# A two-layer hybrid decoder trunk: masked maxima in one operation, a planner with other durations, split weight tiles in places of 4352 bytes

## The chip, the core and the metric

The kernel runs on one core of a Trainium2 chip. The core has a matrix engine (PE; its weight loads are listed apart as PEld), a vector engine (DVE), an activation engine (ACT), a general engine (POOL) and a queue that starts transfers (SP). The metric is device time in microseconds, median of several runs. A profile of one execution gives times for every instruction; all rows below come from it.

## What is computed

```python
for i in range(DEPTH):                     # DEPTH = 2, SEQ = 256, D_MODEL = 1024, D_FF = 2816
    x = x + 0.5 * swiglu(rms_norm(x, ffn1_norm_g[i]), ffn1_w_in[i], ffn1_w_out[i])
    hn = rms_norm(x, mix_norm_g[i])
    if i % N_MIXERS == 0:
        proj = hn @ a_w_in[j]; y_tok = mlstm_heads(...)          # mixer A: 4 heads
    else:
        proj = hn @ b_w_in[j]; y_tok = swa_heads(...)            # mixer B: 16 heads of 64, 2 key heads
    y_mem = memory_heads(xq, mem_k, mem_v, ...)                  # 4 heads over 256 memory rows
    x = x + jnp.concatenate([y_tok, y_mem], axis=-1) @ w_out
    x = x + 0.5 * swiglu(rms_norm(x, ffn2_norm_g[i]), ffn2_w_in[i], ffn2_w_out[i])
```

The change touches the window heads of mixer B. In `swa_heads` each block of 128 queries sees its own keys and those of the block before it, under a mask, with one learned extra logit per head (the sink):

```python
s = jnp.where(valid, jnp.einsum('bqhgd,bkhd->bhgqk', qn, kn), -jnp.inf)
m = jnp.maximum(jnp.max(s, axis=-1, keepdims=True), sink)
p = jnp.exp(s - m)
denom = jnp.sum(p, axis=-1, keepdims=True) + jnp.exp(sink - m)
out = jnp.einsum('bhgqk,bkhd->bqhgd', p / denom, vn)
```

## The kernel before

**Products in three parts.** Every projection is made of float32 values split in a rounded high part and the rest. A weight tile (128 rows by 4 x 256 columns, 512 KB) is fetched by SP into one of five raw tiles `wr`; ACT makes its high part (`round`, line 312, tile `wh`), DVE the rest (`rest`, line 324, tile `wl`). `mm3` then issues high x high, high x low and low x high, 24 matmuls of 256 columns for a weight tile, all at line 456. A matmul has an operand that is loaded into the array (the weights of the instruction) and one that moves through it. In the feed-forward layers, the output projections and part of mixer A's input projection the weight tile is the loaded operand and the activations (`xh`, `xl`, or `u` tiles) move. In the memory stage at the start, in mixer B's input projection and where mixer A needs tokens in rows (`Group(rows=True)`, the gates), it is the other way round: activations are loaded and the weight tile moves.

**Where the tiles lie.** Pools are laid one after another in on-chip memory, in the order of their creation. Weight tile number i of the whole plan goes to pool `whp[i % 2]` and `wlp[i % 2]`, four places of 4096 bytes each; the small pool `gp` (two tiles of 64 bytes) stands between the pools of even and those of odd numbers. Eight temporaries `t` of 2048 bytes follow (pool `tp`).

**The order of the work.** All instructions of all five queues are put in order while the program is built (`manual_schedule`). A small planner, class `Weave`, holds a model clock `now` for PE and one for each other engine. The main line of the program is a generator that issues projection matmuls in pieces of six; everything else (norms, heads, activations) are generators, "chains", which tell by `yield` when they could go on. `pump` lets a chain go on if its time is at most 0.4 us (`LEAD`) ahead of `now`, or not ahead at all if its next step is a matmul. A class `Job` counts what a chain's steps cost: `dve`, `act`, `pool` and `pe`. The order so found is then fixed; on the chip each engine works through its queue and waits on semaphores where the model was wrong.

**A window head of mixer B** (`head`, from line 1422) handles two heads of 64 at once. Per pair it writes the mask into two banks by a bf16 product of an identity with the mask (line 1436, two matmuls of 384 columns), adds the scores on top (line 1441: four matmuls, each recorded as two), takes four negated maxima from the banks (lines 1446 and 1447), combines them with the negated sink (1451, 1452), makes four exponentials from the banks with their sums (1461), frees the banks, normalises (1466, 1467, 1473), transposes the probabilities (through line 470), copies them (1483) and multiplies with the values (1492). Eight such pairs run between the pieces of the projections.

Of the kernel before, what the change touches and what calls it, by code (L numbers as in the profile page):

```python
# [19 lines left out]
P = 128  # L20
# [99 lines left out]
class Job:  # L120


    def __init__(self, wv, *t):
        self.wv, self.eng, self.t = wv, None, max(t, default=wv.now + 0.32)
# [15 lines left out]
    def pe(self):  # L140

        self.wv.now += 0.12
        self.t, self.eng = self.wv.now + 0.3, "pe"
        return self.t
# [3 lines left out]
def tile_trunk(ctx: ExitStack, tc: tile.TileContext, a, out):  # L148
# [13 lines left out]
    mk(cst, [P, 16], F32, "pad")  # L162
# [85 lines left out]
    identb = mk(cst, [P, P], BF16, "identb")  # L248
# [3 lines left out]
    nsink = mk(cst, [P, 16], F32, "nsink")  # L252
# [5 lines left out]
    def late_constants():  # L258
# [8 lines left out]
        nc.vector.tensor_copy(identb, ident)  # L267
# [5 lines left out]
        nc.vector.tensor_scalar(nsink, sink, -1.0, None, op0=ALU.mult)  # L273
# [5 lines left out]
    class Stream:  # L279
# [14 lines left out]
        def fetch(self, i):  # L294
            src, shape, pre = self.plan[i]
# [13 lines left out]
        def round(self, i):  # L309
            shape, j = self.plan[i][1], Job(wv, self.landed[i])  # L310
            self.hi[i] = self.split(whp[i % 2], f"wh{i % 2}", shape)
            nc.scalar.copy(self.hi[i], self.raw[i])  # L312
            self.cast[i] = j.act(shape[1] * shape[2])

        def split(self, pool, tag, shape):

            if shape[2] == GATED:
                return mk(pool, [P, shape[1], 384], F32R, tag)[:, :, :GATED]
            return mk(pool, shape, F32R, tag)

        def rest(self, i):
            shape, j = self.plan[i][1], Job(wv, self.cast[i])
            self.lo[i] = self.split(wlp[i % 2], f"wl{i % 2}", shape)
# [50 lines left out]
    def cols(w, c0, kh):  # L374
        return chunks(w)[:, kh * 4:(kh + 1) * 4, c0:c0 + 256], [P, 4, 256], None

    def row(w, kc):
        return w[kc * P:(kc + 1) * P, :].rearrange("p (a b) -> p a b", a=4), [P, 4, 256], None
# [29 lines left out]
    def mem_plan():  # L408

        o = 0  # L410
        for i, (k0, nk, q0, nq) in enumerate(MEM_TILES):
# [4 lines left out]
            yield src, [P, nk, nq * T], None if pre is None else mem_in(*pre)  # L416

    def ffn_plan(w_in, w_out):
# [4 lines left out]
        for c2 in range(4):  # L423
            for k0, nk in KG:
                yield chunks(w_out)[:, k0:k0 + nk, c2 * 256:(c2 + 1) * 256], [P, nk, 256], None

    def mixer_plan(w, pair, rest, w_out, gates=None):
        for kh in range(2):
            for c0 in pair:
                yield cols(w, c0, kh)  # L430
        for c0 in rest:
            if c0 == gates:
                for k in range(0, 8, 2):
                    yield chunks(w)[:, k:k + 2, c0:c0 + GATED], [P, 2, GATED], None
                continue
            for kh in range(2):
                yield cols(w, c0, kh)
# [6 lines left out]
    for i, (src, shape, _) in enumerate(list(ffn_plan(a["ffn1_w_in"][0], a["ffn1_w_out"][0]))):  # L444
        plan.append((src, shape, x_in(i) if i < 2 else None))
    plan += mixer_plan(a["a_w_in"][0], A_PAIR, A_REST, a["a_w_out"][0], 3072)
    plan += ffn_plan(a["ffn2_w_in"][0], a["ffn2_w_out"][0])
    plan += ffn_plan(a["ffn1_w_in"][1], a["ffn1_w_out"][1])
    plan += mixer_plan(a["b_w_in"][0], B_PAIR, B_REST, a["b_w_out"][0])
# [37 lines left out]
    class Norm:  # L487
# [14 lines left out]
        def put(self, j, c2, xn):  # L502
            hi, lo = mk(xhp, [P, 2, T], F32R, "xh"), mk(xlp, [P, 2, T], F32R, "xl")
            for m in range(2):
                act(hi[:, m], xn[:, m], AF.Copy, scale=g(self.gi + 2 * c2 + m))  # L505
                j.act(T)
            yield j.t
            for m in range(2):
                stt(out=lo[:, m], in0=xn[:, m], scalar=g(self.gi + 2 * c2 + m), in1=hi[:, m].bitcast(F32),
                    op0=ALU.mult, op1=ALU.subtract)  # L510
                j.dve(T)
# [30 lines left out]
        def finish(self, j):  # L542
# [10 lines left out]
            if not self.rows:  # L553
# [5 lines left out]
                yield j.pe()  # L559
# [11 lines left out]
            yield j.pe()  # L571
# [146 lines left out]
    def memory():  # L718
# [73 lines left out]
        def keys(i):  # L792
# [6 lines left out]
            yield j.pe()  # L799
# [19 lines left out]
    def ffn(x, nxt=None, mid=None):  # L819
# [3 lines left out]
        def hidden(gi, bs):  # L823
# [3 lines left out]
            for m in range(2):  # L827
                tt(out=t[:, m], in0=bs[m].t[:, :T], in1=x.rb, op=ALU.mult)  # L828
                j.dve(T)
# [3 lines left out]
            for m in range(2):  # L833
                tt(out=t[:, m], in0=t[:, m], in1=bs[m].t[:, T:], op=ALU.mult)  # L834
                j.dve(T)
# [110 lines left out]
    def cross(src, banks, gi, layer, x, scales, ys, clear=lambda: True):  # L946
# [7 lines left out]
        yield j.pe()  # L954
# [5 lines left out]
        def head(m):  # L960
# [8 lines left out]
            yield j.pe()  # L969
# [3 lines left out]
            for h in range(2):  # L973
                act(p[:, h], sv[:, h], AF.Exp, bias=c[:, 2 + h:3 + h], accum_out=c[:, 4 + h:5 + h])
                j.act(T, True)
# [12 lines left out]
            yield j.pe()  # L988
# [8 lines left out]
            yield j.pe()  # L997
# [55 lines left out]
    def mixer_a(x, nxt):  # L1053
# [46 lines left out]
        def gates():  # L1100
# [15 lines left out]
            yield j.pe()  # L1116
# [40 lines left out]
            yield j.pe()  # L1157
# [24 lines left out]
        def decay(hd):  # L1182
# [24 lines left out]
            yield j.pe()  # L1207
# [30 lines left out]
        def numerators(hd, gr):  # L1238
# [21 lines left out]
            yield j.pe()  # L1260
# [29 lines left out]
            yield j.pe()  # L1290
# [81 lines left out]
    def mixer_b(x, nxt):  # L1372
# [5 lines left out]
        def keys(gr):  # L1378
# [15 lines left out]
            yield j.pe()  # L1394
# [9 lines left out]
        def queries(gi, gr):  # L1404
# [7 lines left out]
            yield j.pe()  # L1412
# [9 lines left out]
        def head(ch, qr):  # L1422
# [12 lines left out]
            for s in sc:  # L1435
                nc.tensor.matmul(s[:, :384], identb, maskb[:, :384], start=True, stop=False, skip_group_check=True)  # L1436
                wv.now += 0.16

            for cs, qs, ks in ((slice(0, P), slice(0, P), slice(0, P)), (slice(P, 384), slice(P, T), slice(0, T))):
                for e in range(2):  # L1440
                    nc.tensor.matmul(sc[e][:, cs], qr[es[e], m, qs], kd[es[e], jh, ks], start=False, stop=True,  # L1441
                                     skip_group_check=True)
                wv.now += (cs.stop - cs.start) * 0.0017
            yield j.pe()
            for e, s in enumerate(sc):
                nc.vector.tensor_reduce(out=c[:, e:e + 1], in_=s[:, :P], axis=AX.X, op=ALU.max, negate=True)
                nc.vector.tensor_reduce(out=c[:, 2 + e:3 + e], in_=s[:, P:384], axis=AX.X, op=ALU.max, negate=True)
                j.dve(P)
                j.dve(T)
# [128 lines left out]
```

## Time and profile before

| | |
|---|---|
| median of 3 runs | 995.66 us (994.76 to 995.8) |
| the profiled execution: its time, its span | 995.73 us, 994.0 us |
| PE busy, matmuls | 987.1 us (99%), 8531 |
| DVE, ACT, POOL busy | 680.0, 512.5, 53.7 us |
| transfers, busy share of 16 engines | 182.75 MB; 56.8% for the main queue |
| granted TensorE clock, mean | 1.000 |

The stages follow each other: memory (0 to 29 us), feed-forward (29 to 222), mixer A (222 to 326), two feed-forward layers (326 to 702), mixer B (702 to 810), feed-forward (to 990). In rows of the profile `bank<-wh,u` means: written is a bank of accumulators, the moving operand is `wh`, the loaded one `u`. A group's row gives the count after `x`, then the busy time and the mean duration in ns, then idle time of the engine before it and who ended it. A row of the timeline gives start, length (to the end of the last of its xN instructions), engine, line, and in brackets idle time before it. Matmuls overlap: one lasts some 277 ns, but a new one starts every 113 or so, so pace is read from starts.

### The profile page before, as it was taken

The numbers are of one execution on the slowest core, as the hardware profiler recorded it, in microseconds if no ns is written. First come the engines' busy times: TensorE is split into PE (matmuls) and PEld (weight loads), VectorE is DVE, ScalarE is ACT, GpSimd is POOL, SyncE is SP. The second block draws the span as 40 slices with busy tenths as digits, with TensorE's granted clock in tenths as the row PEclk, the third lists the DMA queues.
The fourth block names the chain that finished last, engine by engine and source line by source line (L and its number), as shares of the span: only waits on it lengthen the run. The fifth ranks groups of instructions, "written<-read, shape, count | busy, mean of one in ns | idle before, by whom it ended". The sixth has DMA issues, their size and how long they took to land.

```text
span 994.0 us, 20546 instructions
## 1 busy us (share of the span) xinstructions
PE 987.1 (99%) x8531; PEld 972.3 (98%) x8531; DVE 680.0 (68%) x1104; ACT 512.5 (52%) x778; POOL 53.7 (5%) x45
## 2 busy tenths in 40 slices
PE   8999999999999999999999999999999999999998
PEld 7999999999999999999999999999998899999998
DVE  7986666568767586666567776657688788776651
ACT  7754534447656464454444544445566765544440
POOL 1400000001001100000010000001122010000000
PEclk9999999999999999999999999999999999999999
DMA  9776565646455467656665657565523257666650
GB/s 338 223 252 203 172 192 190 190 133 213 145 170 162 156 211 234 192 179 187 195 221 167 198 182 232 171 209 168 185 86 102 95 166 226 219 196 206 192 171 23
DMA packets 169726, 182.75 MB, mean 184 GB/s; under 512 B 6076, under 2 KB 163952, under 8 KB 169632
## 3 DMA queue, kind: packets, MB, share of 16 engines
q1 hardware_dynamic: 168352, 179.63, 56.8%
q0 software_dynamic: 416, 0.75, 0.5%
q8 instruction: 67, 1.10, 0.4%
q10 hardware_dynamic: 864, 1.05, 0.3%
q14 instruction: 27, 0.22, 0.1%
HBM read 180.35 MB, written 1.05 MB: 183 GB/s over the span
## 4 chain that ended last, share of the span: by engine, by line
PE 98%; DMA 1%; ACT 0%; issue 0%; SPq 0%; DVE 0%; DVEq 0%; ACTq 0%
PE bank L456 92%; PE bank L465 2%; PE bank L470 2%; PE bank L1441 1%; PE bank L1492 1%; DMA wr<-in_a_w_in_dram 1%; DMA u<-in_mem_w_kv_dram 1%; PE bank L1436 0%; ACT wh L312 0%; SPq L385 0%; SPq L306 0%; DVE t L911 0%; ACT u L1108 0%; DVEq L1574 0%; ACTq L312 0%
## 5 line engine op out<-in xcount | busy, mean ns | idle before, releaser
L324 DVE TENSOR_TENSOR wl<-wr,wh 128x1024 fp32r<-128x1024 f32 (+1 forms) x346 | 404.5, 1208 | 50.8 <-ACT wh L312 49.5
L456 PE MATMUL bank<-xh,wh 128*128 128x256 f32 x1536 | 426.3, 278 | 0.0
L456 PE MATMUL bank<-xh,wl 128*128 128x256 f32 x1536 | 424.7, 277 | 0.0
L456 PE MATMUL bank<-xl,wh 128*128 128x256 f32 x1536 | 424.7, 277 | 0.0
L312 ACT CAST wh<-wr 128x1024 fp32r<-128x1024 f32 (+1 forms) x346 | 338.8, 1022 | 84.9 <-PE bank L456 48.5
L456 PE MATMUL bank<-u,wh 128*128 128x256 f32 x1792 | 308.3, 278 | 0.0
L456 PEld LDWEIGHTS bank<-xh,wh 128*128 128x128 f32 x1536 | 288.6, 188 | 0.1
L456 PEld LDWEIGHTS bank<-xl,wh 128*128 128x128 f32 x1536 | 288.5, 188 | 0.1
L456 PEld LDWEIGHTS bank<-xh,wl 128*128 128x128 f32 x1536 | 288.4, 188 | 0.0
L456 PEld LDWEIGHTS bank<-u,wh 128*128 128x128 f32 x1792 | 270.0, 188 | 1.7 <-issue 1.7
L456 PE MATMUL bank<-u,wl 128*128 128x256 f32 x896 | 247.9, 277 | 0.0
L456 PEld LDWEIGHTS bank<-u,wl 128*128 128x128 f32 x896 | 168.3, 188 | 0.0
L831 ACT ACTIVATE t<-t 128x512 f32<-128x512 f32 x44 | 27.8, 632 | 172.3 <-DVE t L828 171.7
L828 DVE TENSOR_TENSOR t<-bank,rb 128x256 f32<-128x256 f32 x88 | 35.9, 423 | 74.5 <-PE bank L456 74.5
L456 PE MATMUL bank<-wh,xh 128*128 128x256 f32 (+1 forms) x208 | 60.4, 290 | 0.0
L505 ACT ACTIVATE xh<-u,gcol 128x256 fp32r<-128x256 f32 x48 | 21.6, 501 | 71.3 <-DVE u L894 59.0
L456 PE MATMUL bank<-wl,xh 128*128 128x256 f32 (+1 forms) x208 | 58.2, 280 | 0.0
L456 PE MATMUL bank<-wh,xl 128*128 128x256 f32 (+1 forms) x208 | 58.1, 279 | 0.0
L535 POOL TENSOR_TENSOR u<-u,t 128x512 f32<-128x512 f32 x14 | 24.4, 1743 | 586.1 <-ACT t L532 585.9
L834 DVE TENSOR_TENSOR t<-t,bank 128x256 f32<-128x256 f32 x88 | 32.8, 418 | 24.9 <-ACT t L831 24.8
L891 DVE TENSOR_TENSOR t<-bank,hrb 128x512 f32<-128x512 f32 x12 | 8.3, 692 | 55.6 <-PE bank L456 55.6
L474 ACT CAST u<-t 128x512 fp32r<-128x512 f32 x44 | 27.4, 622 | 31.7 <-DVE t L834 23.3
(194 smaller groups left out, 664.9 us busy)
## 6 DMA issues: line engine op xcount, KB each, us to landing
wr<-in_ffn_w_in_dram SPq DMA_DIRECT2D x176, 512.0 KB, 5.1
wr<-in_ffn_w_out_dram SPq DMA_DIRECT2D x80, 512.0 KB, 4.8
wr<-in_a_w_in_dram SPq DMA_DIRECT2D x26, 512.0 KB, 5.0
wr<-in_b_w_in_dram SPq DMA_DIRECT2D x14, 512.0 KB, 4.9
wr<-in_a_w_out_dram SPq DMA_DIRECT2D x12, 512.0 KB, 4.1
wr<-in_b_w_out_dram SPq DMA_DIRECT2D x12, 512.0 KB, 3.3
wr<-in_ffn_w_out_dram SPq DMA_DIRECT2D x16, 256.0 KB, 3.0
wr<-in_mem_w_kv_dram SPq DMA_DIRECT2D x6, 512.0 KB, 7.0
```

The lines of the kernel that those rows point to most:

```text
L312: nc.scalar.copy(self.hi[i], self.raw[i])
L324: tt(out=self.lo[i], in0=self.raw[i], in1=self.hi[i].bitcast(F32), op=ALU.subtract)
L456: nc.tensor.matmul(ps, lhsT, rhs, start=start, stop=stop, skip_group_check=True)
L465: nc.tensor.matmul(ps, lhsT, rhs, start=start, stop=stop, skip_group_check=True)
L470: nc.tensor.transpose(ps, src, ident[:k, :k])
L474: nc.scalar.copy(hi, src)
L505: act(hi[:, m], xn[:, m], AF.Copy, scale=g(self.gi + 2 * c2 + m))
L535: nc.gpsimd.tensor_tensor(out=self.acc, in0=self.acc, in1=sq, op=ALU.add)
L828: tt(out=t[:, m], in0=bs[m].t[:, :T], in1=x.rb, op=ALU.mult)
L831: act(t, t, AF.Silu)
L834: tt(out=t[:, m], in0=t[:, m], in1=bs[m].t[:, T:], op=ALU.mult)
L1441: nc.tensor.matmul(sc[e][:, cs], qr[es[e], m, qs], kd[es[e], jh, ks], start=False, stop=True, skip_group_check=True)
```

## The change

1. **Window heads.** The two mask matmuls go; the first score matmul of a bank starts it. One DVE operation per block (`tensor_tensor_reduce`) adds the mask, writes the masked scores to the tile that will hold the probabilities, and gives their maximum. The banks are freed at once and the exponentials read that tile. The maxima are no longer negated, so the sink is used as it is and one small operation turns the sign. The tiles `identb` and `nsink` and the two operations that fill them go.
2. **Places of the split weights.** Eight pools of one place each for `wh` and eight for `wl`, tile i in place i % 8; a place is 1088 words (4352 bytes), and the tile starts 32 or 64 words into it, by the parity of i and by whether the plan marks the tile as moving. Six temporaries `t` instead of eight, `gp` moved behind them, and the padding after `onesr` 96 words instead of 16.
3. **The planner.** Other durations for DVE and ACT; a step that depends on the one before pays `HOP` (0.04) on its own engine too, one that does not (`dep=False`) nothing; `pe` adds what its caller gives, from 0.0 to 0.4, instead of 0.12.

```diff
-    def use(self, eng, cost):
-        start = max(self.wv.clock[eng], self.t + (0.0 if eng == self.eng else HOP))
-        self.wv.clock[eng], self.t, self.eng = start + cost, start + cost + 0.08, eng
+    def use(self, eng, cost, dep=True):
+        start = max(self.wv.clock[eng], self.t + HOP if dep else 0.0)
+        self.wv.clock[eng], self.t = start + cost, start + cost + 0.08
         return self.t
-    def dve(self, n=8):
-        return self.use("dve", 0.08 + n * 0.00103)
-    def act(self, n=8, total=False):
-        return self.use("act", 0.14 + n * 0.00092 + 0.09 * total)
+    def dve(self, n=8, dep=True):
+        return self.use("dve", 0.07 + n * 0.00104, dep)
+    def act(self, n=8, total=False, dep=True):
+        return self.use("act", 0.13 + n * 0.0008 + 0.09 * total, dep)
-    def pe(self):
-        self.wv.now += 0.12
+    def pe(self, more):
+        self.wv.now += more
...
-    mk(cst, [P, 16], F32, "pad")
+    mk(cst, [P, 96], F32, "pad")
...
-    whp, wlp = [pool("whp0", 4)], [pool("wlp0", 4)]
+    whp = [pool(f"whp{i}", 1) for i in range(8)]
+    wlp = [pool(f"wlp{i}", 1) for i in range(8)]
+    tp = pool("tp", 6)
+    sp = pool("sp", 2)
     gp = pool("gp", 1)
-    whp.append(pool("whp1", 4))
-    wlp.append(pool("wlp1", 4))
-    tp = pool("tp", 8)
-    sp = pool("sp", 2)
...
+        def split(self, i, pool, tag):
+            shape, moving = self.plan[i][1], self.plan[i][3]
+            n = shape[2] if shape[2] != GATED else 384
+            o = (32, 64)[i % 2] if not moving else (64, 32)[i % 2]
+            w = mk(pool[i % 8], [P, 1088], F32R, tag)[:, o:o + shape[1] * n].rearrange("p (a b) -> p a b", a=shape[1])
+            return w[:, :, :shape[2]]
...
-            yield j.pe()
+            yield j.pe(0.03)
...
-            for s in sc:
-                nc.tensor.matmul(s[:, :384], identb, maskb[:, :384], start=True, stop=False, skip_group_check=True)
-                wv.now += 0.16
...
-                    nc.tensor.matmul(sc[e][:, cs], qr[es[e], m, qs], kd[es[e], jh, ks], start=False, stop=True,
+                    nc.tensor.matmul(sc[e][:, cs], qr[es[e], m, qs], kd[es[e], jh, ks], start=cs.start == 0, stop=True,
                                      skip_group_check=True)
...
-            yield j.pe()
-            for e, s in enumerate(sc):
-                nc.vector.tensor_reduce(out=c[:, e:e + 1], in_=s[:, :P], axis=AX.X, op=ALU.max, negate=True)
-                nc.vector.tensor_reduce(out=c[:, 2 + e:3 + e], in_=s[:, P:384], axis=AX.X, op=ALU.max, negate=True)
-            snk = nsink[:, 2 * ch:2 * ch + 2].unsqueeze(1).to_broadcast([P, 2, 2])
-            tt(out=v22(c[:, 8:12]), in0=v22(c[:, 0:4]), in1=snk, op=ALU.min)
-            tt(out=v22(c[:, 12:16]), in0=v22(c[:, 8:12]), in1=snk, op=ALU.subtract)
+            yield j.pe(0.4)
+            p = [unit(F32).rearrange("p a b -> p (a b)") for _ in range(2)]
+            for e in range(2):
+                for h, cs in BLOCKS:
+                    nc.vector.tensor_tensor_reduce(
+                        out=p[e][:, cs], in0=sc[e][:, cs], in1=maskb[:, cs], scale=1.0, scalar=NEG,
+                        op0=ALU.add, op1=ALU.max, accum_out=c[:, 2 * h + e:2 * h + e + 1])
+                    j.dve(cs.stop - cs.start, e + h == 0)
+                bs[e].free()
+            snk = sink[:, 2 * ch:2 * ch + 2].unsqueeze(1).to_broadcast([P, 2, 2])
+            tt(out=v22(c[:, 8:12]), in0=v22(c[:, 0:4]), in1=snk, op=ALU.max)
+            tt(out=v22(c[:, 12:16]), in0=snk, in1=v22(c[:, 8:12]), op=ALU.subtract)
+            nc.vector.tensor_scalar(c[:, 8:12], c[:, 8:12], -1.0, None, op0=ALU.mult)
...
-                    act(p[e][:, cs], sc[e][:, cs], AF.Exp, bias=c[:, 8 + i:9 + i], accum_out=d[:, 4 + i:5 + i])
-                    j.act(cs.stop - cs.start, True)
-                bs[e].free()
+                    act(p[e][:, cs], p[e][:, cs], AF.Exp, bias=c[:, 8 + i:9 + i], accum_out=d[:, 4 + i:5 + i])
+                    j.act(cs.stop - cs.start, True, e + h == 0)
```

More of the change, by code (lines that the diff above doesn't have):

```diff
@@ L310, in round @@
             shape, j = self.plan[i][1], Job(wv, self.landed[i])
[L311 removed]
+            self.hi[i] = self.split(i, whp, "wh")
             nc.scalar.copy(self.hi[i], self.raw[i])
             self.cast[i] = j.act(shape[1] * shape[2])
[L315 to L319, printed above, removed]
+        def split(self, i, pool, tag):
[4 more added lines that the diff above has]
+            return w[:, :, :shape[2]]
         def rest(self, i):
             shape, j = self.plan[i][1], Job(wv, self.cast[i])
[L323 removed]
+            self.lo[i] = self.split(i, wlp, "wl")
             tt(out=self.lo[i], in0=self.raw[i], in1=self.hi[i].bitcast(F32), op=ALU.subtract)
@@ L433, in mixer_plan @@
                 for k in range(0, 8, 2):
-                    yield chunks(w)[:, k:k + 2, c0:c0 + GATED], [P, 2, GATED], None
+                    yield chunks(w)[:, k:k + 2, c0:c0 + GATED], [P, 2, GATED], None, True
                 continue
             for kh in range(2):
-                yield cols(w, c0, kh)
+                yield cols(w, c0, kh, moving)
         for kc in ORDER + LATE:
@@ L443, in tile_trunk @@
     plan = list(mem_plan())
-    for i, (src, shape, _) in enumerate(list(ffn_plan(a["ffn1_w_in"][0], a["ffn1_w_out"][0]))):
-        plan.append((src, shape, x_in(i) if i < 2 else None))
-    plan += mixer_plan(a["a_w_in"][0], A_PAIR, A_REST, a["a_w_out"][0], 3072)
+    for i, (src, shape, _, moving) in enumerate(list(ffn_plan(a["ffn1_w_in"][0], a["ffn1_w_out"][0]))):
+        plan.append((src, shape, x_in(i) if i < 2 else None, moving))
+    plan += mixer_plan(a["a_w_in"][0], A_PAIR, A_REST, a["a_w_out"][0], (3336, 1024, 1280, 1536, 1792), 3072)
     plan += ffn_plan(a["ffn2_w_in"][0], a["ffn2_w_out"][0])
     plan += ffn_plan(a["ffn1_w_in"][1], a["ffn1_w_out"][1])
-    plan += mixer_plan(a["b_w_in"][0], B_PAIR, B_REST, a["b_w_out"][0])
+    plan += mixer_plan(a["b_w_in"][0], B_PAIR, B_REST, a["b_w_out"][0], B_PAIR + B_REST)
     plan += ffn_plan(a["ffn2_w_in"][1], a["ffn2_w_out"][1])
@@ L1473, in head @@
                     nc.vector.tensor_scalar(p[e][:, cs], p[e][:, cs], d[:, 12 + i:13 + i], None, op0=ALU.mult)
-                    j.dve(cs.stop - cs.start)
+                    j.dve((cs.stop - cs.start) * 0.73, e + h == 0)
             yield from room(j, 2)
```

68 lines of the change are left out of this document (31 added, 37 removed).

## The prediction

> **What bounds the kernel now.** I read the page's head and chain first, then the windows by stage.
>
> ```profile
> span 994.0 us, 20546 instructions
> ...
> PE 98%; DMA 1%; ACT 0%; issue 0%; SPq 0%; DVE 0%; DVEq 0%; ACTq 0%
> ```
> ```profile
> 0.00:43.00 43.00, 40.41 (x322) 37.93 (x323) 35.08 (x59) 33.67 (x56) 13.79 (x15) 1.00 0.86 298
> ...
> 222.00:326.00 104.00, 103.44 (x835) 101.34 (x834) 76.51 (x153) 65.84 (x121) 7.62 (x9) 1.00 0.56 175
> ...
> 701.00:811.00 110.00, 110.00 (x911) 99.97 (x910) 86.44 (x231) 68.98 (x173) 13.91 (x8) 1.00 0.39 124
> ```
>
> The columns after the window's length are busy time of PE, PEld, DVE, ACT and POOL, then the granted clock. The chain is PE almost throughout, at full clock. PE idles 2.59 us of the first 43, 0.56 of mixer A (222 to 326) and nothing of mixer B (701 to 811). There is hardly a wait left to remove: only matmuls that are not issued, or issued closer together, shorten this kernel.
>
> How close they come differs by stage. The chain in order of time gives the feed-forward stages, the timeline of PE the memory stage:
>
> ```profile
> 46.24 175.13 PE bank L456 x1545
> ...
> 316.32 404.19 PE bank L456 x3560
> ...
> 797.94 192.36 PE bank L456 x1694
> ```
> ```profile
> 12.15 1.98 PE L456 MATMUL bank<-wh,u 128*128 128x256 f32 x16
> 13.97 1.07 PE L456 MATMUL bank<-wl,u 128*128 128x256 f32 x8
> 14.88 2.04 PE L456 MATMUL bank<-wh,u 128*128 128x256 f32 x16
> 16.77 1.10 PE L456 MATMUL bank<-wl,u 128*128 128x256 f32 x8
> 17.71 1.98 PE L456 MATMUL bank<-wh,u 128*128 128x256 f32 x16
> 19.53 1.07 PE L456 MATMUL bank<-wl,u 128*128 128x256 f32 x8
> 20.43 2.05 PE L456 MATMUL bank<-wh,u 128*128 128x256 f32 x16
> ```
>
> The operand named first after the arrow moves, the second is loaded as weights. With the weight tile loaded (xh,wh and u,wh) a matmul follows each 175.13/1545 = 113.4 ns. With the weight tile moving (wh,u) it depends on the tile: 24 matmuls take 14.88 - 12.15 = 2.73 us in one tile, 17.71 - 14.88 = 2.83 in the next, 2.72 in the third. Tiles of even number take longer than those of odd number, by 0.10 us a tile or 4.2 ns a matmul. Same shapes, same clock, no idle time: what alternates with a tile's number is its pool, whp[i % 2], and so its start address.
>
> **The change: the mask.** Line 1436's two matmuls a head go.
>
> ```profile
> 741.17 0.28 PE L456 MATMUL bank<-wh,xl 128*128 128x256 f32 x1
> ...
> 742.59 0.50 PE L1436 MATMUL bank<-maskb,identb 128*128 128x384 bf16 x2
> 743.01 0.93 PE L1441 MATMUL bank<-u,u 64*128 64x128 f32 x8
> ```
> ```profile
> 757.18 0.28 PE L456 MATMUL bank<-wl,xh 128*128 128x256 f32 x1
> 757.30 0.28 PE L456 MATMUL bank<-wh,xl 128*128 128x256 f32 x1
> 757.51 0.87 PE L1492 MATMUL bank<-t,u 128*64 128x256 f32 x8
> ```
>
> From 742.59 to 743.01 they hold PE for 0.42 us. Not all of it goes: a matmul on part of the array comes late after one on the whole of it (757.30 to 757.51 is 0.21, where 0.12 is usual), and the scores at line 1441 use 64 rows, so these 0.09 us stay. Eight heads by 0.33 us give **2.7 us**; if the 0.09 went too it would be 3.4, and I take 2.6 as the low end. PE has no idle time there, so all of it shortens the span.
>
> **The mask's other side.** The maxima move to an operation that adds the mask, takes the maximum and writes the masked scores.
>
> ```profile
> L1447 DVE TENSOR_REDUCE col<-bank 128x1 f32<-128x256 f32 x16 | 6.6, 415 | 0.0
> ...
> L1446 DVE TENSOR_REDUCE col<-bank 128x1 f32<-128x128 f32 x16 | 4.6, 286 | 3.6 <-PE bank L1441 3.4
> ...
> L689 DVE TENSOR_SCALAR col<-col,qsc 128x4 f32<-128x4 f32 x8 | 1.4, 224 | 0.0
> ```
> ```profile
> L602 DVE CUSTOM_DVE_ANT_0 t<-rb,con x2: 286/287/288, 221.7 to 221.9; 128x128 f32<-128x128 f32 x2
> L602 DVE DVE_READ_ACCUMULATOR2_ANT rc<- x2: 82/82/82, 221.9 to 222.1; 128x1 f32 x2
> ```
> ```profile
> L828 DVE TENSOR_TENSOR t<-bank,rb 128x256 f32<-128x256 f32 x88 | 35.9, 423 | 74.5 <-PE bank L456 74.5
> ...
> L505 ACT ACTIVATE xh<-u,gcol 128x256 fp32r<-128x256 f32 x48 | 21.6, 501 | 71.3 <-DVE u L894 59.0
> ```
>
> On 128 columns it took 287 + 82 = 369 ns where the reduction takes 286. On 256 from PSUM it is not in this trace: at least 423 + 82 = 505 (a two-input operation of that size plus the accumulator's read), at most twice 369 = 738; I take 505 against 415. With the added sign change at 224 a head costs DVE 2 x 0.083 + 2 x 0.090 + 0.224 = 0.57 us more (at most 1.04), 4.6 in all (8.3). Mixer B leaves DVE 23.6 us idle, but order counts, so look at the wait behind it:
>
> ```profile
> 791.11 1.01 DVE L1473 TENSOR_SCALAR u<-u,col 128x128 f32<-128x128 f32 x4
> ```
> ```profile
> 793.96 0.82 PE L470 MATMUL bank<-con,u 128*128 128x128 f32 x6
> ...
> 797.07 0.87 PE L1492 MATMUL bank<-t,u 128*64 128x256 f32 x8
> 797.87 0.50 PE L456 MATMUL bank<-u,wh 128*128 128x256 f32 x2
> ```
>
> These probabilities are ready at 792.12 and PE turns to them at 793.96, 1.84 us later, filled with output-projection matmuls. A head 0.57 (or 1.04) later still finds cover; without it, eight heads would cost 4.6 us. The last head has more: behind 797.87 come 108 projection matmuls up to 810.4, the last 48 alone needing heads 6 and 7. The exponentials reading SBUF instead of PSUM cost ACT about nothing (501 ns for 256 columns from SBUF); two banks come free before them instead of behind. I cost this part at **0**. The two small operations dropped at the start are off the path.
>
> **The places.** The sizes of the pools give the starts. Modulo 512 bytes a weight tile starts at 0 (even) or 128 (odd) now, the activations at 448. A place becomes 4352 bytes, 256 more than before, so with the offsets of 32 or 64 words a loaded weight tile starts at 128 (even) or 0 (odd), a moving one at 256 or 384. Moving start less loaded start: moving weights had 0 - 448 = 64 (the tiles of 2.83 us) and 128 - 448 = 192 (those of 2.73); loaded weights have 448 and 320, both of which run at 113.4 ns through the 1545 matmuls above. After, moving weights get 256 - 448 = 320 and 384 - 448 = 448, the two that run well today; loaded weights keep 448 and 320. The padding keeps the activations where they are.
>
> ```profile
> L456 PE MATMUL bank<-wh,xh 128*128 128x256 f32 (+1 forms) x208 | 60.4, 290 | 0.0
> ```
> ```profile
> L456 PE MATMUL bank<-wh,u 128*128 128x256 f32 x128 | 17.3, 284 | 1.4 <-ACT wh L312 1.4
> ```
>
> Three products of 208 in the mixers and, one and a half times 128, 192 in the memory stage are 816 matmuls, 34 tiles of 24; the 17 even ones lose 17 x 0.10 = 1.7 us. That is the most to gain; the most to lose is the other 17 turning to that pace, again 1.7. Between interruptions by the heads a stretch need not find the better pace at once, so I take **1.0**, a part of the gain.
>
> Here the Trainium skill speaks against the change. TensorE: Matmul & The Clock Gate, "Step-by-step: what each phase is for", says that PE has two independent SBUF read ports and that loading the next weights takes nothing from the running matmul. By it the places would be worth nothing and the sum would be 993.0; the 2.83 and 2.73 us of neighbouring tiles do not agree with it.
>
> **Six temporaries.** The tightest reuse that I find six places apart is in the memory stage:
>
> ```profile
> 25.33 1.78 DVE L538 TENSOR_TENSOR u<-u,t 128x512 f32<-128x512 f32 x1
> ```
> ```profile
> 29.98 0.62 ACT L532 ACTIVATE t<-u 128x512 f32<-128x512 f32 x1
> ```
>
> The old user ends at 27.11, the new one begins at 29.98: 2.9 us of room, cost **0**.
>
> **The planner's durations** reorder the queues. Turning to a chain counts 0.02 or 0.03 us of PE time instead of 0.12, a dependent step on the same engine 0.04 more than before. Mixer A is where it could hurt:
>
> ```profile
> 248.25 1.07 ACT L990 COPY t<-bank 128x512 f32<-128x512 f32 x2 [1.29 <-PE bank L470]
> ```
> ```profile
> 249.12 0.38 PE L465 MATMUL bank<-t,vM 128*128 128x256 f32 x1
> ```
> ```profile
> 230.01 0.45 PE L470 MATMUL bank<-con,u 128*36 128x128 f32 x2 [0.56 <-ACT u L1108]
> ```
>
> The matmul at 249.12 has half of its input ready only since about 248.8. Eight such turns a quarter of a microsecond late would cost 2 us; the 0.56 us stall at 230.01 may vanish. Bounds -0.6 and +2, value **0**, since the two edits pull in opposite directions.
>
> **The sum** is made against the profiled execution: 995.73 us, 994.0 of span and 1.7 around it, 0.07 above the median of 995.66. 995.73 - 2.7 - 1.0 = **992.0**.
>
> **Rivals.** *Only the mask pays*: if starts count modulo 256 and not by distance, moving weights at 256 and 384 behave as at 0 and 128: 993.0. For it: nothing in this trace starts at 256 modulo 512. Against: distance sorts all four cases seen. *More than forecast*: the whole 3.4 and 1.7, the 0.56, and the 1.21 us that PE waits at 7.85 for its second tile: 988.9. *The planner takes back part*: 2 us of new turns, 994.0, or somewhat more. *Slower*: the feed-forward stages fall into the pace of 2.83 us a tile. They are 1545 + 3560 + 1694 = 6799 matmuls; at 4.2 ns half of them would cost 14 us, 1006. Against it: their distances do not change, only even and odd swap. It decides once some 57 tiles of 24 run so (57 x 0.10 is over the 3.7 saved plus 2).
>
> ```profile
> 7.85 1.22 PE L456 MATMUL bank<-wh,u 128*128 128x256 f32 x8 [1.21 <-ACT wh L312]
> ```
>
> **Chances.** Forecast 0.46, mask alone 0.21, more 0.10, planner's loss 0.15, slower 0.08. This kernel's measurement can tell about 0.2% (2 us) from no change: below 993.7 is faster, above 997.7 slower. The forecast and "more" are faster, of mask alone most (0.17); with rounding faster 0.73, same 0.19, slower 0.08. The range is 988.9 to 996.0: low end the larger gain, high end the planner's loss with the moving tiles' 1.7 lost too (995.73 - 2.7 + 2 + 1.7 = 996.7, cut to 996.0 as all at once is unlikely).
>
> **What would show it.** Line 1436 gone and 0.33 us less from a projection matmul to the first score; the memory tiles all near 2.73 us; feed-forward at 113.4 ns; PE idle in 701 to 811 still near zero although DVE has 4 to 5 us more. Wrong if a tile at 256 or 384 still takes 2.83, if transposes of the probabilities wait for DVE, or if mixer A shows new idle time on PE.

## The result, and the profile after

The changed kernel takes 998.00 us (median of 9 runs, 996.83 to 998.75) against 995.51 us of the kernel before (9 runs beside them, 994.73 to 995.92). The ratio is 1.0026, with a 95% interval of 1.0017 to 1.0035: slower by a quarter of a per cent, where 992.0, a gain of 3.7 us, was forecast. The profiled execution took 997.94 us. Its page begins:

```profile
span 996.2 us, 20547 instructions
## 1 busy us (share of the span) xinstructions
PE 985.2 (99%) x8515; PEld 972.1 (98%) x8515; DVE 682.1 (68%) x1142; ACT 513.8 (52%) x778; POOL 51.6 (5%) x45
```

PE is busy 1.9 us less than before (987.1), and the span is 2.2 us longer. So PE stands idle 4.1 us more. The windows of the same three stages say where (columns as before: length, busy PE, PEld, DVE, ACT, POOL, granted clock):

```profile
0.00:43.00 43.00, 39.67 (x319) 37.07 (x320) 34.56 (x56) 33.15 (x56) 14.69 (x18) 1.00 0.83 283
...
222.00:326.00 104.00, 104.00 (x843) 102.14 (x842) 76.80 (x155) 66.56 (x122) 8.38 (x9) 1.00 0.54 173
...
701.00:811.00 110.00, 106.02 (x871) 97.68 (x870) 85.53 (x266) 68.73 (x168) 12.14 (x8) 0.98 0.38 122
```

Mixer B, where PE had no idle time at all, now has 3.98 us of it, and its clock is no longer 1.00. Mixer A lost its 0.56 us stall. In the first 43 us PE idles 3.33 us instead of 2.59; new there is one wait, not in the memory stage but behind it, in the first feed-forward layer, where a sum waits for a `u` tile that DVE makes late:

```profile
32.13 0.62 PE L455 MATMUL bank<-onesr,u 128*128 128x256 f32 x3 [0.81 <-DVE u L475]
```

The timeline of PE in the changed kernel shows the waits of mixer B (in brackets: idle time before the row, and who ended it):

```profile
771.96 0.28 PE L455 MATMUL bank<-u,wl 128*128 128x256 f32 x1
772.16 1.58 PE L1437 MATMUL bank<-u,u 64*128 64x128 f32 x16
773.68 0.50 PE L455 MATMUL bank<-u,wh 128*128 128x256 f32 x2
...
775.92 0.87 PE L1492 MATMUL bank<-t,u 128*64 128x256 f32 x8 [1.27 <-DVE col L1445]
...
777.62 0.55 PE L469 MATMUL bank<-con,u 128*128 128x128 f32 x3 [0.35 <-DVE col L1445]
...
781.56 0.55 PE L469 MATMUL bank<-con,u 128*128 128x128 f32 x3 [2.35 <-DVE u L475]
...
783.10 2.76 PE L1492 MATMUL bank<-t,u 128*64 128x256 f32 x16
...
791.45 1.52 PE L1492 MATMUL bank<-t,u 128*64 128x256 f32 x16
```

Look at who ends each wait. Line 1492 multiplies the probabilities (`t`) with the values (`u`). It does not read what line 1445, the masked maximum of another head, makes. What it takes from line 1445 is the *bank* that the maximum still reads. The transposes at 781.56 likewise need no result of line 475: that is the reader of a finished output bank. The timeline of DVE gives the same times from the other side:

```profile
775.44 0.42 DVE L1445 CUSTOM_DVE_ANT_0 u<-bank,maskb 128x256 f32<-128x256 f32 x1
...
777.14 0.42 DVE L1445 CUSTOM_DVE_ANT_0 u<-bank,maskb 128x256 f32<-128x256 f32 x1
...
779.03 1.01 DVE L1473 TENSOR_SCALAR u<-u,col 128x128 f32<-128x128 f32 x4
779.95 1.22 DVE L323 TENSOR_TENSOR wl<-wr,wh 128x1024 fp32r<-128x1024 f32 x1
781.09 0.42 DVE L475 TENSOR_TENSOR u<-bank,u 128x256 fp32r<-128x256 f32 x1
```

The reads of the maxima end at 775.86 and 777.56, and PE starts 0.06 us after each. Line 475 ends at 781.51, PE starts at 781.56. The values of that output bank were finished at 776.79 (775.92 + 0.87), but its reader came 4.3 us later, behind the maxima of another head, a normalisation and the rest of a weight tile.

After that the clock drops. The windows around it (the clock is the column before the transfers' share):

```profile
778.00:782.00 4.00, 1.65 (x15) 1.41 (x14) 3.33 (x13) 0.96 (x2) 0.00 (x0) 1.00 0.00 2
782.20:785.60 3.40, 3.40 (x22) 2.34 (x20) 1.02 (x6) 3.18 (x15) 0.00 (x0) 0.51 0.47 153
786.00:790.00 4.00, 4.00 (x37) 4.00 (x37) 2.99 (x9) 3.34 (x9) 0.00 (x0) 1.00 0.33 97
```

For 3.4 us PE has half its clock, which costs about 1.7 us; the sixteen matmuls at 783.10 take 2.76 us where those at 791.45 take 1.52.

The account of the span, from these windows: idle in mixer B +3.98, half clock +1.7, the first 43 us +0.74, mixer A -0.56, together +5.86. The span grew by 2.2, so 3.7 us came off elsewhere. That the forecast had the same 3.7 for the mask and the places together (2.7 + 1.0) does not show that each was right; how much is each is for the experiments.

Two more readings, of the memory stage's timeline and of the chain through the feed-forward layers:

```profile
14.36 2.05 PE L455 MATMUL bank<-wh,u 128*128 128x256 f32 x16
...
17.19 1.98 PE L455 MATMUL bank<-wh,u 128*128 128x256 f32 x16
...
19.92 2.05 PE L455 MATMUL bank<-wh,u 128*128 128x256 f32 x16
```
```profile
315.85 404.08 PE bank L455 x3560
```

Weight tiles still alternate, 2.83 and 2.73 us, as before. The feed-forward layers run at 404.08/3560 = 113.5 ns, as before.

### The profile page after: what moved, and what is told of

It reads as the page before. It is cut to its first block, busy times and chain, and to the rows that moved or that the text cites. A ratio compares the mean times of both kernels' runs of the same rounds, so it can differ in the third digit from the quotient of the medians.

```text
span 996.2 us, 20547 instructions
## 1 busy us (share of the span) xinstructions
PE 985.2 (99%) x8515; PEld 972.1 (98%) x8515; DVE 682.1 (68%) x1142; ACT 513.8 (52%) x778; POOL 51.6 (5%) x45
## 4 chain that ended last, share of the span: by engine, by line
PE 95%; DVE 3%; DMA 1%; ACT 0%; issue 0%; SPq 0%; DVEq 0%; ACTq 0%
PE bank L455 90%; PE bank L464 2%; PE bank L469 1%; DVE wl L323 1%; DMA u<-in_xT_dram 1%; PE bank L1492 1%; DMA wr<-in_mem_w_kv_dram 1%; PE bank L1437 0%; DVE u L1445 0%; DVE u L1473 0%; DVE xl L508 0%; SPq L303 0%; ACT wh L309 0%; SPq L384 0%; ACT xh L504 0%
```

## Theories and experiments

**A, banks.** The planner gives a bank back (`free_banks.append`) when its reader has been *queued*, not when it has run. Before the change the score banks were handed back behind the exponentials, that is after a `yield` up to the planned end of the maxima; now they are handed back the moment the maxima are queued. PE then takes a bank whose reader stands deep in DVE's queue. **B, durations.** The planner's new costs are wrong (a score turn counts 0.4 us, a value turn 0.35) and the order is worse for it. **C, load.** DVE has too much work in mixer B. Against C speaks the table of groups already (count after x, then busy us and mean ns):

```profile
L1445 DVE CUSTOM_DVE_ANT_0 u<-bank,maskb 128x256 f32<-128x256 f32 x16 | 6.7, 420 | 0.0
L1445 DVE CUSTOM_DVE_ANT_0 u<-bank,maskb 128x128 f32<-128x128 f32 x16 | 4.6, 286 | 1.5 <-PE bank L1437 1.5
L1445 DVE DVE_READ_ACCUMULATOR2_ANT col<- 128x1 f32 x32 | 2.7, 83 | 0.0
L1453 DVE TENSOR_SCALAR col<-col 128x4 f32<-128x4 f32 x8 | 1.4, 170 | 0.3
```

The masked maxima take as long as the plain ones did (420 and 286 ns against 415 and 286); new are the accumulator reads, 2.7 us, and the sign change, 1.4 us. DVE's busy time grew by 2.1 us in all (680.0 to 682.1), less than the 4.6 forecast, because the reads overlap the next operation.

The kernel before was measured beside each group: 995.1 us in the first (31 runs), 995.06 in the second (20 runs), 994.90 in the third (29 runs), 994.96 in the fourth (30 runs). Idle time is PE's in mixer B (701 to 811; in k8 the stage lies later, and its idle time is left out). The change's 998.00 is the median of the result above, against 995.51 beside it.

| kernel | us | ratio, 95% interval | idle, us |
|---|---|---|---|
| before | 995.1 | 1 | 0.00 |
| the change | 998.00 | 1.0026 [1.0017, 1.0035] | 3.98 |
| k1: score banks handed back later | 993.54 | 0.9986 [0.9977, 0.9996] | 1.13 |
| k2: smaller counts for the turns | 995.84 | 1.0010 [1.0000, 1.0019] | 1.94 |
| k3: masked maxima alone | 995.19 | 1.0002 [0.9993, 1.0011] | 2.46 |
| k4: the same, banks later | 994.72 | 0.9996 [0.9986, 1.0005] | 2.25 |
| k5: places alone | 994.39 | 0.9993 [0.9984, 1.0003] | 0.00 |
| k6: planner alone | 998.61 | 1.0035 [1.0022, 1.0048] | 2.66 |
| k7: places, all distances 192 | 994.71 | 0.9997 [0.9987, 1.0006] | 0.00 |
| k8: places, all distances 64 | 1018.15 | 1.0153 [1.0133, 1.0174] | |
| m1: the change, timed banks | 992.53 | 0.9977 [0.9966, 0.9987] | 0.00 |
| m2: masked maxima alone, timed banks | 993.03 | 0.9981 [0.9971, 0.9990] | 1.51 |
| m3: before, timed banks | 995.22 | 1.0001 [0.9992, 1.0011] | 0.05 |
| m4: planner alone, timed banks | 996.84 | 1.0020 [1.0011, 1.0030] | 0.75 |
| n1: the change without the planner | 994.94 | 1.0000 [0.9991, 1.0009] | 2.39 |
| n2: the same, timed banks | 992.54 | 0.9977 [0.9968, 0.9986] | 1.35 |
| n3: the change, timed banks, old turn counts | 993.43 | 0.9988 [0.9979, 0.9997] | 0.69 |
| m5: new durations alone, old turn counts | 997.31 | 1.0024 [1.0014, 1.0033] | 1.03 |

### When the score banks come back (k1, k2)

k1 moves the hand-back of the two score banks behind the next `yield`; k2 changes two numbers of the change.

```diff
 # k1
-                bs[e].free()
 ...
             yield j.dve()
+            for q in bs:
+                q.free()
             act(d[:, 0:4], c[:, 12:16], AF.Exp)
 # k2
-            yield j.pe(0.4)
+            yield j.pe(0.2)
...
-            yield j.pe(0.35)
+            yield j.pe(0.25)
```

> The changed kernel, but a head's two score banks are given back one step later, when the maxima are planned to be done, instead of as soon as they are queued. Theory A (banks): PE stands 3.98 us in mixer B because it takes a bank whose reader on DVE is queued but not yet done. Then PE's idle time in mixer B falls below 0.5 us, the 3.4 us at half clock go too, and the time is 998.0 - 4.0 - 1.7 = 992.3 (991.3 to 993.5). Theory B (the planner counts too much PE time for the heads, 0.4 and 0.35): idle time stays above 3 us, 997 to 999. Theory C (DVE's extra 0.57 us a head is what is late): idle time stays, 997 to 999.

> The changed kernel with the planner's counts for the two steps of a window head lowered to what the trace shows, 0.4 to 0.2 and 0.35 to 0.25; banks as in the changed kernel. Theory B: PE no longer runs ahead of its plan, idle time in mixer B below 1 us, 992 to 994. Theory A: the order changes a little but banks are still taken early; idle time 2 to 6 us and 996 to 1000.

k1, the window of mixer B:

```profile
701.00:811.00 110.00, 108.87 (x913) 101.41 (x912) 89.91 (x274) 72.42 (x177) 13.96 (x10) 1.00 0.37 121
```

Waits for line 1445 are gone; 1.13 us remain, both pieces behind line 475 and its output banks. The instructions are the same, only their order is not, and the kernel goes from 1.0026 to 0.9986. That is what theory A says, though more idle time is left than the 0.5 us that it allowed. k2 took off half of the idle time as well and brought 1.0010; its 1.94 us lie between what B (below 1) and A (2 to 6) had said. Any shift of the plan moves the waits, but those that remain in k2 are still for the readers of score banks:

```profile
PE bank L469 <- DVE col L1445: 1.9, 2, 1.3
```

### The three parts alone (k3 to k6)

k3 is the kernel before with part 1 of the change, k4 adds k1's edit, k5 is part 2 alone (mask and planner as before), k6 part 3 alone, with 0.2 and 0.25 for the two large turn counts since the mask's matmuls stand there.

> The kernel before with the masked maxima alone (old places, eight temporaries, old durations; score banks given back as soon as the maxima are queued). Theory A: PE idles 2 to 6 us in mixer B, so the 2.7 us of the mask are lost: 994 to 1000. Theory B: the old counts are in place, so no idle time, 992.8 (995.5 - 2.7). Theory C: idle time as in the changed kernel, 997 to 999.

> As the run with the masked maxima alone, but the score banks are given back when the maxima are planned to be done. Theory A: no idle time on PE in mixer B, 995.5 - 2.7 = 992.8 (992 to 994). Theory C: DVE's extra work still makes PE idle by some 4 us, 997 to 999. Theory B says as without the later giving back.

> The kernel before with the new places and six temporaries alone. If the pace of a moving weight tile goes by its start modulo 512 bytes, as the prediction had it: 994.5, memory tiles all at 2.73 us. If it goes modulo 256: starts of 256 and 384 are as 0 and 128 were, tiles alternate between 2.83 and 2.73 us as before, 995.5 (995.0 to 996.0).

> The kernel before with the planner's new durations alone (the two steps of a window head counted at 0.2 and 0.25, as the mask matmuls are in place again). If the planner's durations by themselves cost time: PE idle time in the mixers above 1 us, 997 or more. If it is the early giving back of banks that does (theory A): 995.5, between 994.5 and 996.5.

The differences of the parts, 995.19, 994.39 and 998.61 against 995.1, are +0.1, -0.7 and +3.5: together 998.0, what the whole change measures. (With banks handed back later the parts do not add up so, as n2 and m1 below show.) The masked maxima alone already give their gain back. The waits on PE in mixer B, of k3 and then of k4 (total, times, longest):

```profile
PE bank L469 <- DVE col L1445: 1.7, 2, 1.2
PE bank L455 <- DVE u L475: 0.6, 1, 0.6
```
```profile
PE bank L469 <- DVE u L475: 2.3, 2, 1.8
```

Two of k3's three waits are for score banks. The third, on line 455, is for data: the output projection needs the low part of a head's output, which line 475 makes. In k4 the waits for the score banks went, but others came behind line 475, of transposes this time: output banks are handed back in the same way. So it is not the score banks only, and k4's 994.72 misses the 992 to 994 of theory A. k6 has no masked maxima at all and, against what was expected of theory A, waits too, for the exponentials that read score banks and for the reader of a query's bank:

```profile
PE bank L473 <- DVE u L701: 1.8, 1, 1.8
PE bank L1439 <- ACT u L1465: 0.8, 2, 0.6
```
```profile
771.09 0.69 DVE L701 TENSOR_TENSOR u<-bank,col 128x512 f32<-128x512 f32 x1
```

The last row, of k6's timeline of DVE, shows that line 701 reads a bank; the transposes that wait for its end (771.78) start at 771.84 and are those of probabilities, which have nothing of line 701 in them.

### The distances (k7, k8)

On k5, one number for all tiles instead of two by parity. k7 makes every distance (moving start less loaded start, modulo 256) 192, k8 makes it 64.

```diff
-            o = (32, 64)[i % 2] if not moving else (64, 32)[i % 2]
+            o = 32 if moving else 64        # k7
+            o = 64 if moving else 32        # k8
```

> As the run with the places alone, but every moving weight tile starts at 128 modulo 256 bytes and every loaded one at 0 (with activations at 192: moving start less loaded start is 192 modulo 256 throughout). If the distance modulo 256 decides and 192 is the good one: memory tiles all at 2.73 us, 17 tiles by 0.10 = 1.7 us less, and somewhat more from stretches with loaded weights that recover sooner: 993.3 (992.5 to 994.3). If places count for nothing: 995.5.

> The opposite of the run before: moving weight tiles at 0, loaded ones at 128 modulo 256 bytes, so the distance is 64 throughout. If the distance decides: all 34 moving tiles at 2.83 us (+1.7), and the feed-forward stages, which enter in the poor pace from the stage before, do not recover on tiles at this distance: up to 6800 x 4.2 ns = 28 us more, so 998 to 1025. If only a moving start of 0 is bad: +1.7 alone, 997.2. If places count for nothing: 995.5.

The memory stage of k5, then of k7:

```profile
12.15 2.04 PE L459 MATMUL bank<-wh,u 128*128 128x256 f32 x16
...
14.97 2.05 PE L459 MATMUL bank<-wh,u 128*128 128x256 f32 x16
...
17.80 2.04 PE L459 MATMUL bank<-wh,u 128*128 128x256 f32 x16
```
```profile
11.84 1.98 PE L459 MATMUL bank<-wh,u 128*128 128x256 f32 x16
...
14.56 1.98 PE L459 MATMUL bank<-wh,u 128*128 128x256 f32 x16
...
17.28 1.98 PE L459 MATMUL bank<-wh,u 128*128 128x256 f32 x16
```

In k5 every tile takes 2.82 or 2.83 us: the new places, alone, did not bring one tile of that stage to 2.73. They need not be what took it from the tiles that had it, for runs in the old places lose it too. m3 below is the kernel before with another order of work, and none of its tiles alternates:

```profile
12.02 2.04 PE L463 MATMUL bank<-wh,u 128*128 128x256 f32 x16
...
14.84 2.05 PE L463 MATMUL bank<-wh,u 128*128 128x256 f32 x16
...
17.67 2.04 PE L463 MATMUL bank<-wh,u 128*128 128x256 f32 x16
```

With one distance of 192, all take 2.72; no other run has that. But k7 pays elsewhere: its last feed-forward layer runs at 193.37/1694 = 114.1 ns, and no gain can be measured. With one distance of 64, in the execution that was profiled, the feed-forward layers themselves fall into the poor pace, 190.01/1612 = 117.9 ns, against 183.19/1612 = 113.6 in k5. First k5, then k7, then k8, from the chain in order of time:

```profile
46.51 183.19 PE bank L459 x1612
```
```profile
795.91 193.37 PE bank L459 x1694
```
```profile
46.70 190.01 PE bank L459 x1612
```

k8's four runs took 1010.31, 1010.74, 1025.56 and 1025.85 us. The ratio of 1.0153 is that of the two shorter ones, and the profile is of the longest, so the pace of each stage in the shorter ones is not known.

### Every bank at the counted end of its reader (m1 to m4)

Now theory A in full, for all banks: a bank goes back to the planner when the model clock reaches the end of the work that was queued last.

```diff
-        def free(self):
-            free_banks.append(self.i)
+        def free(self, early=0):
+            def give():
+                yield (wv.last + 0.7 * early,)
+                free_banks.append(self.i)
+            wv.spawn(give(), 0.0)
```

`use` sets `wv.last` to the end of the step it counts; in the last layer's output, where a bank is freed ahead of its reader's count, `early` adds 0.7 us.

> The changed kernel in which every bank, not the score banks alone, is given back in the planner at the counted end of the work that reads it, instead of when that work is queued. Theory A (PE takes banks whose readers on DVE or ACT are queued and not done) says that the two waits left in mixer B by giving back the score banks later (0.74 and 0.39 us, for the bank of the output) go as well: PE idles under 0.3 us in mixer B, 992.4 (991.5 to 993.3). If instead the new durations cost time of themselves: 993.5 or more, idle time in mixer B as with the score banks alone.

> The masked maxima alone, old places and durations, with every bank given back at the counted end of its readers. Theory A: the 2.46 us of idle time that the masked maxima alone have in mixer B go, 995.2 - 2.4 = 992.8 (992.0 to 993.6). If DVE's extra work is what is late: idle time stays above 1.5 us and the time at 995.

> The kernel before with every bank given back at the counted end of its readers, nothing else. It has no wait for a bank in mixer B to lose, so theory A says no gain: 995.1 (994.3 to 995.9). A gain of 1 us or more here would mean that the new way of giving back banks shortens the kernel by something else than these waits.

> The planner's new durations alone, with every bank given back at the counted end of its readers. Theory A: the 2.66 us of idle time in mixer B of the new durations alone are waits for banks and go, 998.6 - 2.7 = 995.9 (995.0 to 996.7). If the new durations are too short for the exponentials and the like: idle time above 1.5 us stays, 997 or more.

m1, the window of mixer B:

```profile
701.00:811.00 110.00, 110.00 (x921) 102.40 (x920) 91.22 (x274) 73.29 (x179) 14.91 (x10) 1.00 0.37 122
```

No idle time, full clock, with the same work on DVE (682.4 us in all, 682.1 in the change; the 91.22 here are more because more of the stage falls into the window): theory C falls for the change. The whole change with timed banks is faster than both kernels, 0.9977: a gain of 2.4 us, where 3.7 were forecast. The kernel before gains nothing by timed banks (m3), so it is no gain for any order: it takes away what the change brought in. m2 puts a price on the mask, m3 less m2: 995.22 - 993.03 = 2.2 us, with 1.51 us of new idle time in mixer B in it. The longer piece of that is no wait for a bank:

```profile
792.24 0.39 PE L459 MATMUL bank<-u,wh 128*128 128x256 f32 x1 [1.14 <-DVE u L479]
```

The output projection waits here for data, the low part of a head's output that line 479 makes; DVE itself had waited 1.11 us for ACT ahead of it, so this is no sign of too much work on DVE. In no run with timed banks (m1 to m4, n2, n3) is a wait of PE for a bank left in mixer B that the profile shows; those that are left are for what DVE makes. m4 left a question: the planner's part alone kept 1.6 us (996.84 - 995.22) even with timed banks.

### The planner beside the other parts (n1 to n3, m5)

n1 is the change with the planner's part taken out, n2 that with timed banks. n3 is m1, and m5 is k6, with 0.12 us for every turn.

```diff
     def pe(self, more):
-        self.wv.now += more
+        self.wv.now += 0.12             # n3, m5
```

> The change with the planner's old durations and turn costs; masked maxima and new places stay. If the loss comes from the planner's part, the others add up: 995.1 + 0.1 (mask alone) - 0.7 (places alone) = 994.5 (993.6 to 995.4), with 2 to 2.5 us of idle time on PE in mixer B as in the mask alone. If the masked maxima with the early banks are by themselves the loss and the planner only happens to be dear alone: 997 to 998.5, with over 3.5 us idle in mixer B.

> The run before, with every bank given back at the counted end of its readers. If the planner's durations cost 1.6 to 1.9 us even with such banks (as in the planner alone with timed banks, 996.84 against the 995.22 of the kernel before with timed banks): 990.8 (990.3 to 991.3), clearly below the 992.53 of the whole change with timed banks. If that cost does not exist beside the other two parts: 992.3 (991.8 to 993.2), no different from it.

> The whole change with timed banks, but every turn to a chain counted at the old 0.12 us of PE time; the new durations of DVE and ACT stay. If the lower turn costs are what the planner's part still loses: 991 (990.3 to 991.8). If it is the durations, or nothing is lost there: 992.5 (992 to 993.5).

> The planner's new durations of DVE and ACT alone on the kernel before, every turn counted at the old 0.12 us. If the low turn costs make the waits of the planner alone (998.61, 2.66 us idle in mixer B): idle there below 0.5 us and 995.1 (994.3 to 996.0). If the durations make them: over 1.5 us idle there and 997 to 999.

n1 stands at 1.0000, the change at 1.0026: the planner's part is what turns "no gain" into "slower". n2 and m1 are equal (992.54 and 992.53): beside the other two parts and with timed banks, the planner's durations cost nothing on balance. m1 idles 1.35 us less than n2 in mixer B and 0.66 us more in the first 43 us, where the wait for line 475 stays (0.58 us in m1, none in n2). So in the change the planner's part is paid for through banks taken too early. n1 still waits 2.39 us in mixer B, of which most is for score banks and the rest, as in k3, for data:

```profile
PE bank L469 <- DVE col L1445: 1.7, 2, 1.3
PE bank L455 <- DVE u L475: 0.6, 1, 0.6
```

m5 lies between the two expectations in idle time, 1.03 us, but its 997.31 us is in the range of the second, so the durations of DVE and ACT carry the larger part of k6's loss, 2.35 of 3.5 us. n3's old turn counts gained nothing (993.43 against 992.53).

**What stays open.** Why the planner's part alone keeps 1.6 us with timed banks in the old places (m4), when it costs nothing in the new ones. Of it 0.70 us is idle time in mixer B (0.75 less m3's 0.05). The rest lies ahead of mixer B and is not idle time in the first 43 us (2.83 us in m4, 2.86 in m3): m4's chain of the middle feed-forward layers begins at 316.80, m3's at 315.70. For it I have no run. And what besides the starts sets the pace of a weight tile.

## Why the prediction was wrong, point by point

Two terms that the sum had at 0 failed: the mask's other side and the planner. Both cost PE waits for banks.

- **The mask, -2.7: a little low.** Line 1436 is gone. A head that stands alone saves what was forecast: from the start of the last projection matmul ahead of it to the next one behind it 1.40 us before (766.82 to 768.22), 1.06 now (762.48 to 763.54), 0.34 less where 0.33 was said. Two heads in a row save 0.98 us, not 0.66: 2.70 before (741.17 to 743.87), 1.72 now (771.96 to 773.68). Between them there is no turn to the whole array and back any more, which the forecast kept for every head. Four single heads and two pairs make 3.3 us, where eight times 0.33 is 2.6. m2 nets 2.2 us and still waits 1.5.

The start of the two heads before and the projection matmul that follows them, from the timeline of PE:

```profile
741.30 0.50 PE L1436 MATMUL bank<-maskb,identb 128*128 128x384 bf16 x2
...
743.87 0.39 PE L456 MATMUL bank<-wh,xh 128*128 128x256 f32 x1
```

- **The mask's other side, 0: the step that failed.** The prediction measured the cover of the probabilities (1.84 us between their end and the transposes) and wrote "two banks come free before them instead of behind" as if it were harmless. The operand did have cover: in the change no transpose waits for the probabilities of its own head. But a matmul needs an operand *and* a bank, and the edit moved the hand-back of the banks ahead of their reading. k1 undoes that alone: 1.0026 to 0.9986, about 4 us. Beside the old durations the same undoing shows no gain (k3 1.0002, k4 0.9996), since the waits pass to the output banks; there it takes all banks timed to get the mask's gain, 993.03 in m2.
- **DVE's 4.6 us: too high, and beside the point.** The masked maximum of 256 columns took 420 + 83 = 503 ns, the forecast 505, but the reads overlap the next operation, so DVE's busy time grew by 2.1 us.
- **The places, -1.0: not shown.** Alone 0.9993 [0.9984, 1.0003], -0.7 us, which can't be told from nothing. The rule "distance modulo 512" failed: moving tiles at 320 and 448 alternate as those at 64 and 192 did, which is what the rival with period 256 said. Nor is that rule enough: with the same starts every tile is at 2.83 in k5, and in m3 with the starts of before.
- **The planner, 0, bounds -0.6 and +2: outside the bounds, and the other step that failed.** The 0.56 us stall of mixer A went as said. But the loss was looked for in mixer A, and came in mixer B and the first 43 us; taken out of the change the part is worth 0.0026 of the time, 2.6 us, and alone it costs 3.5. The prediction asked which matmuls would find their input late, and not which banks would be handed out early.
- **Six temporaries, 0: no wait of k5 or n1 is new in the memory stage,** where the tightest reuse was looked for.
- **The rival on the slower side** (feed-forward at 2.83 us a tile) did not happen here, yet k8 shows it is real, and in its profiled execution at the price that it was given: 6.8 us in the first feed-forward layer (190.01 - 183.19), where 1612 matmuls by 4.2 ns are 6.8.
- **The rule on two read ports** that the prediction set against the places (the Trainium skill, TensorE: Matmul & The Clock Gate, "Step-by-step: what each phase is for") would have the places worth nothing anywhere. k8's 1.0153 against 0.9993 in k5, by a start of 128 bytes more or less, differs from it.

The half clock was in no part of the forecast. In the profiled execution it comes behind the waits, and adds about 1.7 us to them.

## What to carry to other kernels

Where an order is fixed at build time, a buffer is best given back at the counted *end* of its last reader. A hand-back at queueing did no harm in the kernel before (m3 gains nothing), but an edit that "frees earlier" or changes the counted durations can turn it into waits on a buffer, not on data. When a wait's releaser makes nothing that the waiting instruction reads, look for the buffer it holds. A cover measured for an operand says nothing of the second thing that the instruction needs.

## What the runs showed of the hardware that was not expected

- **The clock can fall to half after short idle times.** In the change 3.97 us of idle time in three pieces within 7 us (774.65 to 781.56, the longest 2.35) were followed by 3.4 us at a clock of 0.51. In k2's profiled execution two pieces of 1.32 and 0.59 us came before 778.56; these are the windows behind them:

```profile
778.00:780.00 2.00, 1.44 (x7) 1.39 (x8) 1.83 (x14) 0.93 (x2) 0.00 (x0) 0.63 0.25 100
780.00:782.00 2.00, 2.00 (x12) 2.00 (x12) 2.00 (x5) 0.51 (x2) 0.00 (x0) 0.52 0.00 0
```

  In k6 pieces of 0.55 and 1.82 us, ending at 765.56 and 771.84, were followed by none. So no rule of lengths comes out of these runs, and it differs between executions of one kernel: of the change's nine, seven show a mean clock of 0.997 or 0.998 (996.93 to 998.75 us), two show 1.000 (996.83 and 997.03).
- **The pace of a 256-column matmul does not follow from shapes, clock and start addresses alone.** It is 113.5 or 117.9 ns in stretches without idle time. k5 and the changed kernel put their tiles at the same starts, and one keeps the poor pace through the memory stage while the other alternates; the kernel before and m3 differ in the same way. Behind the poor memory stages of k5 and m3 the feed-forward layers still ran at 113.6 ns; with one distance of 64 everywhere they stayed at 117.9 in the profiled execution, and k8's four runs of one program lie 15 us apart in two pairs.
